# High-part casts and half of the second-key one-hots on ScalarE, every retrieval dot product on VectorE, and one-hot operands laid out by token pairs

## The chip, the core and the metric

The kernel runs on one NeuronCore of a Trainium2 chip. The core has five engines with an instruction queue each: TensorE (PE in the profile, its weight loads PEld), VectorE (DVE), ScalarE (ACT), GpSimd (POOL) and SyncE (SP), which issues plain DMA transfers. Each engine works through its queue strictly in the order in which the program was written. The metric is the device time of one launch in microseconds (us), the median of several runs.

## The reference

The block takes 512 tokens of width 1024 through a gated token mixer (a pooling branch and a gated delta rule with 8 heads) and then through PEER, a feed-forward layer of 16384 experts with one neuron each. The change touches PEER and the conversions of weights:

```python
q = (x @ w_query).reshape(b, s, 8, 2, 128)
s1 = einsum("bshc,hkc->bshk", q[..., 0, :], keys_1)   # 128 first keys for each head
s2 = einsum("bshc,hkc->bshk", q[..., 1, :], keys_2)   # 128 second keys
v1, i1 = top_k(s1, 16);  v2, i2 = top_k(s2, 16)
# 256 candidate sums v1 + v2, the best 16 of them; expert = i1 * 128 + i2
gates = softmax(top_score)
u  = take(expert_down, experts);  act = gelu(einsum("td,thkd->thk", x, u))
vv = take(expert_up, experts);    y = einsum("thk,thkd->td", gates * act, vv)
out = rmsnorm(h + y)
```

For each token 8 heads pick 16 experts each: 128 pairs of a first and a second key with a gate.

## The kernel before

**Two ways through PEER.** The tokens run in two segments, tokens 0 to 127 and tokens 128 to 511 (`SEGMENTS`, line 59). For the first 256 tokens (two tiles of 128) `retrieve` (line 1020) fetches the rows of the chosen experts: GpSimd issues an indirect DMA of 128 rows (512 KB) for each of the 128 picks, first from `down`, then from `up`. A `down` row goes into a dot product with the token (`tensor_tensor_reduce` on VectorE, CUSTOM_DVE in the profile); an `up` row is added to the tile `hbuf` with its weight (`scalar_tensor_tensor`). Only four buffers `rows` hold fetched rows. In the first tile, `SHARED` gives one dot product in sixteen, eight in all, to GpSimd (a product) and ScalarE (its sum).

**The dense way.** The last 256 tokens go through all 16384 experts (`dense`, line 1056), 128 experts at a time, in 128 steps. A step loads 512 KB of `downt` and 512 KB of `up`; `activations` (line 1093) multiplies the tokens with the first and applies Gelu, `add_up` (line 1110) multiplies by the gates and adds the product with the second into four accumulators. 28 steps of the first kind and 32 of the second take fp32 operands as they are. In the others `split` (line 561) makes a high part (`whi`, a cast to fp32r) and a low part (`wlo`, the difference, on VectorE), and TensorE runs three fp32r products for one. A high part may be cast by ScalarE or VectorE. There are three buffers each for `whi` and `wlo`.

**One-hots.** `gates_of_experts` (line 1062) builds the gate of every expert for every token with products of one-hot matrices, four tokens (`HOTS`) at a time: `o2` [pick, 128 second keys, 4 tokens] says which second key a pick has, `o1` [pick, 4 kinds, N first keys, 4 tokens] holds the same for a range of N first keys and that times the three bf16 pieces of the gate. For each token TensorE loads `o2[:, :, k]` and streams `o1[:, u, :, k]`, three matmuls. Neighbouring columns of these operands lie 4 elements, 8 bytes, apart. It runs in three passes (`PASSES`, line 33): 48 first keys before the dense steps begin, 32 between steps 17 and 46, 48 between steps 48 and 78, each of 64 groups of four tokens. VectorE makes a group in three instructions (`is_equal` for `o2`, `is_equal` for `o1`, a product).

**What sets the order.** The program first records all operations, then `Order.schedule` (line 287) lays them out with a cost for each kind of operation (`_cost`, line 243), a due time (`nc.vt`) and the state of the buffers, and writes each engine's queue in that order. Where `either` (line 202) names two engines, the planner picks one. Any change of a cost or an engine can therefore move instructions all over the program.

Of the kernel before, what the change touches and what calls it, by code (L numbers as in the profile page):

```python
# [13 lines left out]
BF16 = mybir.dt.bfloat16  # L14
I32 = mybir.dt.int32
U32 = mybir.dt.uint32
# [5 lines left out]
P = 128  # L22
# [14 lines left out]
HOTS = 4  # L37
# [11 lines left out]
WHOLE = range(16,80,2)  # L49
SHARED = ((1, 1, 1, 1, 1, 1, 1, 1), (0, 0, 0, 0, 0, 0, 0, 0))  # L50
BIASES = (1, 0.8, 0.6, -0.2, 1.5)
# [461 lines left out]
def block_kernel(ctx: ExitStack, tc: tile.TileContext, x, win, wbd, poolw, wpu, wdn, wmo, wq, down, up, downt,  # L513
# [25 lines left out]
    def psum():  # L539
        return bank([P, 512])  # L540
# [20 lines left out]
    def split(src, dst):  # L561
        copy(dst[0], src)
        if len(dst) == 1:
            return
        hi, lo = dst
        if src.slot.psum:
            nc.vector.tensor_tensor(lo, src, hi.bitcast(F32), op=ALU.subtract)
        else:
            sub(lo, src, hi.bitcast(F32))
# [23 lines left out]
    nc.gpsimd.iota(pari, pattern=[[0, P]], base=0, channel_multiplier=1)  # L593
    rowx = const([P, P, HOTS], BF16)
    nc.vector.tensor_copy(rowx, rowi[:, :, None].to_broadcast([P, P, HOTS]))
    masks = []
# [275 lines left out]
    def finish_tokens(t0, T, mg, exact):  # L872
# [41 lines left out]
        for c in range(16):  # L914
# [12 lines left out]
            for j in range(NT):  # L927
# [4 lines left out]
                top16(sc, VI[j][:, 0, c, :], VI[j][:, 1, c, :].bitcast(U32))  # L932
        bT = const([P, 5, TB], BF16) if any(kept) else None
        for j in range(first):
            vt, nc.vt = nc.vt, max(nc.vt, LATE) if any(kept) else nc.vt
            found = select(VI[j][:, 0], VI[j][:, 1].bitcast(U32), None)
            retrieve(t0 // P + j, *found, x2[j], hs[j])
            nc.vt = vt
        for j in range(first, NT):
            select(VI[j][:, 0], VI[j][:, 1].bitcast(U32), bT[:, :, (j - first) * P:(j - first + 1) * P])  # L940
        if any(kept):
            return bT, hs[first:], x2w[1], parted

# [7 lines left out]
    def select(V, I, slots):  # L951
# [39 lines left out]
        if slots is None:  # L991
            pt, idx = psum()[:, :P], keep([P, P], I32)
            for k in range(2 * TOPK):
                nc.tensor.matmul(pt, times[k // TOPK], hits[k // TOPK][:, k % TOPK, :],
                                 start=k == 0, stop=k == 2 * TOPK - 1)
            nc.vector.tensor_copy(idx, pt)
            return idx, gate
        for s in range(2):
            pt = psum()[:, :P]
            for k in range(TOPK):  # L1000
                nc.tensor.matmul(pt, hits[s][:, k, :], times[1], start=k == 0, stop=k == TOPK - 1)
            copy(slots[:, s, :], pt)
        pt = psum()[:, :P]
        nc.tensor.transpose(pt, gate, ident)
# [15 lines left out]
    def retrieve(j, idx, gate, x2, h):  # L1020
        act, co, shared = keep([P, P]), keep([P, P]), SHARED[j]

# [18 lines left out]
        for b in range(P // GROUP):  # L1041
            pace(b)
            for e in range(b * GROUP, (b + 1) * GROUP):
                row = gather(down, e)
                if e % GROUP * shared[b] // GROUP != (e % GROUP + 1) * shared[b] // GROUP:
                    nc.gpsimd.tensor_tensor(row, row, x2, op=ALU.mult)
                    nc.scalar.activation(row, row, AF.Copy, accum_out=act[:, e:e + 1])
                    continue
                nc.vector.tensor_tensor_reduce(out=row, in0=row, in1=x2, scale=1.0, scalar=0.0,
                                               op0=ALU.mult, op1=ALU.add, accum_out=act[:, e:e + 1])  # L1050
            if b:
                spread(b - 1)
# [3 lines left out]
    def dense(bT, hs, plain, x2w):  # L1056
# [4 lines left out]

        def gates_of_experts(first, N, n, place, *_):
            pieces = [pair([P, PIECE, TB]) if q < n else quads([P, PIECE, TB], at=place) for q in range(N // PIECE)]
# [3 lines left out]
            for t1 in range(0, TB, tb):  # L1067
                pg = bank([P, tb, N])
                for t in range(t1, t1 + tb, HOTS):
                    ts = slice(t, t + HOTS)  # L1070
                    o1, o2 = scr([P, 4, N, HOTS], BF16), scr([P, P, HOTS], BF16)
                    nc.vector.tensor_tensor(o2, rowx, bT[:, 1, None, ts].to_broadcast([P, P, HOTS]), op=ALU.is_equal)
                    nc.vector.tensor_tensor(o1[:, 0], rowx[:, first:first + N, :],
                                            bT[:, 0, None, ts].to_broadcast([P, N, HOTS]), op=ALU.is_equal)
                    nc.vector.tensor_tensor(o1[:, 1:], o1[:, 0:1].to_broadcast([P, 3, N, HOTS]),
                                            bT[:, 2:5, None, ts].to_broadcast([P, 3, N, HOTS]), op=ALU.mult)
                    for k in range(HOTS):
                        for u in range(1, 4):
                            nc.tensor.matmul(pg[:, t - t1 + k, :], o2[:, :, k], o1[:, u, :, k], start=u == 1, stop=u == 3)
                banks.append(len(nc.ops) - 1)  # L1080
# [43 lines left out]
        for e in range(NKEYS):  # L1124
            for k, (first, N, n, place, begin, end) in enumerate(PASSES):
                if e == begin:
                    build.append(gates_of_experts(first, N, n, place))
                if begin <= e <= end:
# [246 lines left out]
```

## Time and profile before

| what | value |
|---|---|
| median of 3 runs | 1857.65 us (1850.95 to 1860.94) |
| profiled execution | 1861.2 us, span of its instructions 1859.4 us |
| TensorE busy, granted clock | 1735.3 us (93%), 0.963 |
| VectorE busy | 1576.5 us (85%) |
| GpSimd busy | 771.0 us (41%) |
| ScalarE busy | 704.6 us (38%) |
| DMA | 509.31 MB, mean 274 GB/s |

The second segment begins at about 200 us. From about 250 us on the retrieval of the first tile runs beside it. The key scores and the selection of the last three token tiles lie between 750 and 966 us. The three one-hot passes run on TensorE from 966 to 1046 us, 1108 to 1297 us and 1313 to 1530 us; the dense steps go on to 1828 us, and beside them the second tile is retrieved.

Busy times of one engine count a moment once, even where its instructions overlap. A group line of the profile gives the busy time of all its instructions, the mean duration of one, and the idle time of the engine just before them with what ended it. All operations are issued through one helper, so that every one of them has line L494; the names of the tiles tell them apart.

### The profile page before, as it was taken

How to read it: one execution, taken by the hardware profiler on the slowest of the kernel's cores; microseconds unless marked ns; L12 is line 12 of the kernel's file. 1: busy time of each engine (PE TensorE's matmuls, PEld its weight loads, DVE VectorE, ACT ScalarE, POOL GpSimd, SP SyncE). 2: the span in 40 equal slices, each digit the busy share in tenths (PEclk: the TensorE clock that was granted, in tenths of full speed). 3: DMA queues.
4: the chain of work that ended last, by engine and by line, in shares of the span. 5: the costliest groups of instructions: out<-in, count | busy, mean ns of one | idle time of the engine just before them, and what ended most of it. 6: DMA issues, size and time to landing. Idle time of an engine off the chain costs nothing.

```text
span 1859.4 us, 33378 instructions
## 1 busy us (share of the span) xinstructions
PE 1735.3 (93%) x12122; PEld 1497.1 (81%) x12122; DVE 1576.5 (85%) x3832; ACT 704.6 (38%) x1688; POOL 771.0 (41%) x607
## 2 busy tenths in 40 slices
PE   7999999999999999899959998899999999999992
PEld 7999789999998874788748865687788878898981
DVE  5531398988987776899979999898999999999996
ACT  6741247747534220321213432233334433232331
POOL 0010026565556555533252254444554455334354
PEclk9999999998999999999979999899999999999996
DMA  7438757576677999877576599888998999999996
GB/s 247 153 120 281 252 187 254 182 255 199 210 242 242 335 318 356 294 237 262 192 251 198 169 372 316 315 289 321 327 336 321 327 320 355 317 333 348 333 353 235
DMA packets 144741, 509.31 MB, mean 274 GB/s; under 512 B 16961, under 2 KB 21185, under 8 KB 144577
## 3 DMA queue, kind: packets, MB, share of 16 engines
q0 software_dynamic: 73728, 268.47, 42.1%
q1 hardware_dynamic: 70848, 238.72, 36.6%
q8 instruction: 95, 1.56, 0.3%
q14 instruction: 70, 0.57, 0.1%
HBM read 505.02 MB, written 2.10 MB: 273 GB/s over the span
## 4 chain that ended last, share of the span: by engine, by line
PE 41%; DVE 21%; issue 15%; DMA 12%; POOL 8%; ACT 3%; POOLq 0%; SPq 0%; DVEq 0%; ACTq 0%
PE bank L494 41%; POOL rows L494 7%; DMA rows<-in_up_dram,keep 6%; DMA rows<-in_down_dram,keep 4%; DVE quad L494 4%; DVE rows L494 4%; DVE wlo L494 3%; DVE hbuf L494 3%; DVE scr L494 3%; DVE sel L494 2%; ACT L494 1%; DMA wraw<-in_win_dram 1%; DMA wraw<-in_downt_dram 1%; ACT scr L494 1%; DMA sel<-in_wq_dram 1%
## 5 line engine op out<-in xcount | busy, mean ns | idle before, releaser
L494 PE MATMUL bank<-xwide,whi 128*128 128x256 f32 (+1 forms) x2432 | 553.5, 313 | 0.9 <-DVE whi L494 0.7
L494 POOL DMA_INDIRECT rows<-in_down_dram,keep x256 | 316.9, 1238 | 474.8 <-DVE keep L494 340.3
L494 POOL DMA_INDIRECT rows<-in_up_dram,keep x256 | 360.5, 1408 | 361.1 <-DVE hbuf L494 198.5
L494 PEld LDWEIGHTS bank<-xwide,whi 128*128 128x128 f32 x2432 | 416.9, 195 | 8.7 <-issue 2.2
L494 PE MATMUL bank<-xwide,wlo 128*128 128x256 f32 (+1 forms) x1216 | 379.3, 312 | 13.9 <-DVE wlo L494 13.0
L494 ACT CAST whi<-wraw 128x512 fp32r<-128x512 f32 x406 | 251.0, 621 | 328.8 <-PE bank L494 269.1
L494 DVE SCALAR_TENSOR_TENSOR hbuf<-rows,keep,hbuf 128x1024 f32<-128x1024 f32 x256 | 329.8, 1288 | 45.7 <-DMA rows<-in_up_dram,keep 44.5
L494 DVE TENSOR_TENSOR wlo<-wraw,whi 128x512 fp32r<-128x512 f32 x496 | 341.9, 704 | 15.4 <-ACT whi L494 13.6
L494 DVE CUSTOM_DVE_ANT_0 rows<-rows,xbuf 128x1024 f32<-128x1024 f32 x248 | 304.3, 1232 | 43.2 <-DMA rows<-in_down_dram,keep 42.9
L494 PE MATMUL bank<-pair,wraw 128*128 128x128 f32 (+1 forms) x1728 | 259.5, 304 | 3.0 <-ACT pair L494 1.3
L494 PEld LDWEIGHTS bank<-xwide,wlo 128*128 128x128 f32 x1216 | 237.1, 195 | 26.1 <-DVE wlo L494 21.1
L494 PEld LDWEIGHTS bank<-pair,wraw 128*128 128x128 f32 x1728 | 223.0, 196 | 27.3 <-ACT pair L494 1.6
L494 PE MATMUL bank<-whi,xwide 128*128 128x512 f32 x768 | 238.4, 397 | 2.4 <-DVE xwide L494 0.9
L494 PE MATMUL bank<-quad,wraw 128*128 128x256 f32 x704 | 175.8, 394 | 0.0
L494 PEld LDWEIGHTS bank<-whi,xwide 128*128 128x128 f32 x768 | 138.7, 189 | 33.4 <-DVE xwide L494 2.9
L494 PE MATMUL bank<-wlo,xwide 128*128 128x512 f32 x384 | 147.2, 399 | 3.8 <-DVE wlo L494 3.6
L494 PEld LDWEIGHTS <-scr 128*128 128x128 bf16 x2304 | 110.5, 118 | 46.9 <-issue 31.8
L494 PEld LDWEIGHTS bank<-quad,wraw 128*128 128x128 f32 x704 | 130.1, 196 | 17.6 <-issue 3.0
L494 PE MATMUL bank<-scr 128*128 128x48 bf16 (+1 forms) x2304 | 120.5, 214 | 15.5 <-DVE scr L494 14.6
L494 DVE TENSOR_TENSOR scr<-c,c 128x512 bf16<-128x512 bf16 (+2 forms) x384 | 114.2, 330 | 5.3 <-PE bank L494 4.3
L494 POOL TENSOR_TENSOR small<-small,c 128x1 f32<-128x1 f32 (+1 forms) x20 | 22.2, 1109 | 181.1 <-DVE small L494 93.7
L494 PE MATMUL bank<-wraw,acts 128*128 128x512 f32 x208 | 96.2, 602 | 0.0
(160 smaller groups left out, 2081.6 us busy)
## 6 DMA issues: line engine op xcount, KB each, us to landing
wraw<-in_downt_dram SPq DMA_DIRECT2D x128, 512.0 KB
wraw<-in_up_dram SPq DMA_DIRECT2D x128, 512.0 KB
wraw<-in_win_dram SPq DMA_DIRECT2D x104, 512.0 KB
wraw<-in_wq_dram SPq DMA_DIRECT2D x32, 512.0 KB
wraw<-in_wdn_dram SPq DMA_DIRECT2D x16, 512.0 KB
wraw<-in_wmo_dram SPq DMA_DIRECT2D x16, 512.0 KB
wraw<-in_wpu_dram SPq DMA_DIRECT2D x8, 512.0 KB
rows<-in_down_dram,keep POOLq DMA_INDIRECT x256
```

Source lines behind the costliest of these rows:

```text
L494: ins = getattr(getattr(self.nc, eng), meth)(*(real(a) for a in args), **{k: real(a) for k, a in kw.items()})
```

## The change

`split` casts the high part on ScalarE always. `SHARED` is gone, so that all 256 dot products run on VectorE. `rowx`, `o1` and `o2` hold the tokens by pairs, so that neighbouring columns of an operand lie 2 elements, 4 bytes, apart; the product for `o1` becomes two instructions, one for each pair. In every second group (`SHARE`, 8 of 16) ScalarE makes `o2`: for each token |second key − row| by `Abs` with the key as bias, and then one `Relu` of 1 − that over the whole group. For it `select` leaves the second keys in fp32 as well (`bF`).

```diff
-SHARED = ((1, 1, 1, 1, 1, 1, 1, 1), (0, 0, 0, 0, 0, 0, 0, 0))
+SHARE = (8, 8, 8)
...
     def split(src, dst):
-        copy(dst[0], src)
+        nc.scalar.copy(dst[0], src)
...
+        slots, wide_slot = slots
         for s in range(2):
...
             copy(slots[:, s, :], pt)
+            if s:
+                copy(wide_slot, pt)
...
                 row = gather(down, e)
-                if e % GROUP * shared[b] // GROUP != (e % GROUP + 1) * shared[b] // GROUP:
-                    nc.gpsimd.tensor_tensor(row, row, x2, op=ALU.mult)
-                    nc.scalar.activation(row, row, AF.Copy, accum_out=act[:, e:e + 1])
-                    continue
                 nc.vector.tensor_tensor_reduce(out=row, in0=row, in1=x2, scale=1.0, scalar=0.0,
...
+        def pairwise(ap, n):
+            rows_of = ap.rearrange("p u (g t) -> p u g t", t=2)
+            return rows_of[:, :, :, None, :].to_broadcast([P, ap.shape[1], HOTS // 2, n, 2])
...
-                    o1, o2 = scr([P, 4, N, HOTS], BF16), scr([P, P, HOTS], BF16)
-                    nc.vector.tensor_tensor(o2, rowx, bT[:, 1, None, ts].to_broadcast([P, P, HOTS]), op=ALU.is_equal)
-                    nc.vector.tensor_tensor(o1[:, 0], rowx[:, first:first + N, :],
-                                            bT[:, 0, None, ts].to_broadcast([P, N, HOTS]), op=ALU.is_equal)
-                    nc.vector.tensor_tensor(o1[:, 1:], o1[:, 0:1].to_broadcast([P, 3, N, HOTS]),
-                                            bT[:, 2:5, None, ts].to_broadcast([P, 3, N, HOTS]), op=ALU.mult)
+                    o1, o2 = scr([P, HOTS // 2, 4, N, 2], BF16), scr([P, HOTS // 2, P, 2], BF16)
+                    if t // HOTS * share // 16 != (t // HOTS + 1) * share // 16:
+                        for k in range(HOTS):
+                            nc.scalar.activation(o2[:, k // 2, :, k % 2], rowx[:, :, 0], AF.Abs, scale=-1.0,
+                                                 bias=bF[:, t + k:t + k + 1])
+                        nc.scalar.activation(o2, o2, AF.Relu, scale=-1.0, bias=1.0)
+                    else:
+                        nc.vector.tensor_tensor(o2, rowx[:, None].to_broadcast([P, HOTS // 2, P, 2]),
+                                                pairwise(bT[:, 1:2, ts], P)[:, 0], op=ALU.is_equal)
+                    nc.vector.tensor_tensor(o1[:, :, 0], rowx[:, None, first:first + N, :].to_broadcast([P, HOTS // 2, N, 2]),
+                                            pairwise(bT[:, 0:1, ts], N)[:, 0], op=ALU.is_equal)
+                    for k in range(HOTS // 2):
+                        nc.vector.tensor_tensor(o1[:, k, 1:], o1[:, k, 0:1].to_broadcast([P, 3, N, 2]),
+                                                pairwise(bT[:, 2:5, ts], N)[:, :, k], op=ALU.mult)
                     for k in range(HOTS):
                         for u in range(1, 4):
-                            nc.tensor.matmul(pg[:, t - t1 + k, :], o2[:, :, k], o1[:, u, :, k], start=u == 1, stop=u == 3)
+                            nc.tensor.matmul(pg[:, t - t1 + k, :], o2[:, k // 2, :, k % 2], o1[:, k // 2, u, :, k % 2],
+                                             start=u == 1, stop=u == 3)
```

The planner lays out a new order. Three places of it follow. In their names `c_86` is `rowx`, `c_106` is `bT` and `c_107` is `bF`; `ISA rows,keep<-rows,xbuf` is a dot product of the retrieval.

VectorE, the end of the selection for the last token tile. Before, after the `RECIPROCAL` of the softmax:

```order
L494 TENSOR_REDUCE small<-sel 128x8
L494 TENSOR_TENSOR scr<-c_86,c_106 128x192
L494 RECIPROCAL small<-small 128x8
L494 ISA rows,keep<-rows,xbuf 128x1024
L494 ISA keep 128x1
...
L494 SCALAR_TENSOR_TENSOR hbuf<-rows,keep,hbuf 128x1024 x2
L494 TENSOR_TENSOR keep<-sel,small 128x128
L494 SCALAR_TENSOR_TENSOR hbuf<-rows,keep,hbuf 128x1024
L494 CAST c_106<-sel 128x128
```

Now:

```order
L494 TENSOR_REDUCE small<-sel 128x8
L494 SCALAR_TENSOR_TENSOR quad<-sel 128x128 x15
L494 RECIPROCAL small<-small 128x8
L494 TENSOR_TENSOR scr<-c_86,c_106 128x2x96
L494 TENSOR_TENSOR keep<-sel,small 128x128
L494 TENSOR_TENSOR scr<-c_86,c_106 128x2x96 x2
L494 SCALAR_TENSOR_TENSOR hbuf<-rows,keep,hbuf 128x1024
L494 CAST c_106<-sel 128x128
```

Before, twelve dot products of the first tile and two additions stood between the reciprocal and the gate (`keep<-sel,small`); now one one-hot does, and all 128 dot products of that tile stand ahead of the selection of the last tile.

ScalarE, in the first one-hot pass. Before, its queue held the three copies that move a finished group of gates out of PSUM, and now and then a Gelu:

```order
L494 ACTIVATE quad<-bank 128x256
L494 COPY pair<-bank 128x16x8 x6
L494 ACTIVATE quad<-bank 128x256
L494 COPY pair<-bank 128x16x8 x9
L494 ACTIVATE quad<-bank 128x256
```

Now:

```order
L494 ACTIVATE scr<-c_86,c_107 128x128 x4
L494 COPY pair<-bank 128x16x8 x3
L494 ACTIVATE scr<-scr 128x512
L494 ACTIVATE scr<-c_86,c_107 128x128 x3
L494 ACTIVATE quad<-bank 128x256
L494 ACTIVATE scr<-c_86,c_107 128x128
L494 COPY pair<-bank 128x16x8 x3
L494 ACTIVATE scr<-scr 128x512
```

Between two sets of three copies stand four `Abs` and a `Relu`.

VectorE, the end of the program. Before:

```order
L494 COPY wraw<-bank 128x512
L494 SCALAR_TENSOR_TENSOR hbuf<-rows,keep,hbuf 128x1024
L494 TENSOR_SCALAR small<-small 128x1
L494 SCALAR_TENSOR_TENSOR hbuf<-rows,keep,hbuf 128x1024 x7
L494 SCALAR_TENSOR_TENSOR wraw<-wraw,small,rows 128x1024
L494 SCALAR_TENSOR_TENSOR xbuf<-hbuf,small,rows 128x1024
```

Now:

```order
L494 SCALAR_TENSOR_TENSOR xbuf<-hbuf,small,rows 128x1024
L494 TENSOR_TENSOR wlo<-wraw,whi 128x512 x2
L494 TENSOR_TENSOR acts<-acts,quad 128x256
L494 TENSOR_TENSOR xwide<-acts,xwide 128x256
L494 TENSOR_TENSOR wlo<-wraw,whi 128x512 x4
L494 COPY wraw<-bank 128x512 x4
L494 SCALAR_TENSOR_TENSOR wraw<-wraw,small,rows 128x1024 x2
```

The retrieved tile's last step (`xbuf<-hbuf`) was the last instruction of all; now it stands ahead of the last low parts of the dense steps, and the dense tokens end the queue.

## Rows read from the trace of the kernel before

**Rows 1.** The page, busy time of each engine over the span.
```profile
PE 1735.3 (93%) x12122; PEld 1497.1 (81%) x12122; DVE 1576.5 (85%) x3832; ACT 704.6 (38%) x1688; POOL 771.0 (41%) x607
```

**Rows 2.** Windows: us, busy by engine (instructions), granted clock, DMA share, GB/s.
```profile
650.00:700.00 50.00, 49.11 (x206) 36.73 (x205) 37.03 (x44) 9.72 (x16) 27.76 (x21) 1.00 0.91 323
966.00:1046.00 80.00, 76.51 (x930) 67.50 (x931) 76.69 (x208) 25.18 (x108) 18.93 (x15) 0.91 0.54 173
1046.00:1828.00 782.00, 751.03 (x5314) 614.77 (x5312) 757.90 (x1489) 280.37 (x631) 364.94 (x262) 0.98 0.92 326
1108.00:1297.00 189.00, 174.39 (x1448) 131.76 (x1448) 178.53 (x408) 57.31 (x127) 82.53 (x68) 0.95 0.88 312
1297.00:1530.00 233.00, 229.41 (x1840) 184.98 (x1839) 225.99 (x459) 92.71 (x240) 115.30 (x81) 1.00 0.93 328
1530.00:1700.00 170.00, 166.54 (x1029) 145.88 (x1026) 167.33 (x296) 57.61 (x120) 76.41 (x55) 0.99 0.94 340
1828.00:1859.00 31.00, 0.00 (x0) 0.00 (x0) 16.31 (x17) 3.63 (x7) 11.64 (x9) 0.51 0.65 232
```

**Rows 3.** Timeline around the selection's end: start, us, instruction, [idle before and releaser].
```profile
929.66 0.20 DVE L494 RECIPROCAL small<-small 128x8 f32<-128x8 f32 x1
941.95 1.23 DVE L494 CUSTOM_DVE_ANT_0 rows<-rows,xbuf 128x1024 f32<-128x1024 f32 x1 [3.29 <-DMA rows<-in_down_dram,keep]
...
962.17 0.28 DVE L494 TENSOR_TENSOR keep<-sel,small 128x128 f32<-128x128 f32 x1
...
962.50 0.47 PE L494 MATMUL bank<-c,keep 128*128 128x128 f32 x1 [13.63 <-DVE keep L494]
```

**Rows 4.** Timeline of PE: one-hot matmuls, each run with its follower, and fp32r matmuls.
```profile
1005.82 0.73 PE L494 MATMUL bank<-scr 128*128 128x48 bf16 x12
1006.37 0.68 PE L494 MATMUL bank<-quad,wraw 128*128 128x256 f32 x2
...
1033.09 0.28 PE L494 MATMUL bank<-xwide,wlo 128*128 128x256 f32 x1
1033.21 0.40 PE L494 MATMUL bank<-xwide,whi 128*128 128x256 f32 x2
...
1157.15 0.55 PE L494 MATMUL bank<-scr 128*128 128x32 bf16 x12
1157.55 0.48 PE L494 MATMUL bank<-whi,xwide 128*128 128x512 f32 x1
```

**Rows 5.** Groups by form: count | busy us, mean ns | idle before and releasers.
```profile
L494 DVE TENSOR_TENSOR scr<-c,c 128x512 bf16<-128x512 bf16 x192 | 80.2, 419 | 5.3 <-PE bank L494 4.3
L494 DVE TENSOR_TENSOR scr<-scr,c 128x576 bf16<-128x576 bf16 x128 | 57.2, 449 | 0.0
L494 DVE TENSOR_TENSOR scr<-scr,c 128x384 bf16<-128x384 bf16 x64 | 22.3, 349 | 0.0
L494 DVE TENSOR_TENSOR scr<-c,c 128x192 bf16<-128x192 bf16 x128 | 32.3, 252 | 0.0
L494 DVE CAST whi<-wraw 128x512 fp32r<-128x512 f32 x90 | 38.1, 428 | 6.2 <-PE bank L494 5.0 <-DMA wraw<-in_downt_dram 1.2
L494 DVE CUSTOM_DVE_ANT_0 rows<-rows,xbuf 128x1024 f32<-128x1024 f32 x248 | 304.3, 1232 | 43.2 <-DMA rows<-in_down_dram,keep 42.9
L494 POOL TENSOR_TENSOR rows<-rows,xbuf 128x1024 f32<-128x1024 f32 x8 | 19.5, 2434 | 7.5 <-DMA rows<-in_down_dram,keep 7.5
L494 ACT CAST whi<-wraw 128x512 fp32r<-128x512 f32 x406 | 251.0, 621 | 328.8 <-PE bank L494 269.1 <-DMA wraw<-in_up_dram 14.8 <-issue 11.0
L494 ACT ACTIVATE quad<-quad,small 128x128 f32<-128x128 f32 x16 | 5.3, 389 | 0.0
L494 ACT ACTIVATE quad<-quad 128x512 f32<-128x512 f32 x8 | 5.0, 626 | 0.4 <-DVE quad L494 0.4
L494 ACT COPY pair<-bank 128x128 f32<-128x128 f32 x160 | 33.2, 272 | 97.7 <-PE bank L494 97.5
```

**Rows 6.** Timeline, the end of the program.
```profile
1845.65 2.65 DVE L494 SCALAR_TENSOR_TENSOR hbuf<-rows,keep,hbuf 128x1024 f32<-128x1024 f32 x2 [2.97 <-DMA rows<-in_up_dram,keep]
...
1852.70 0.33 SPq L494 DMA_DIRECT2D out_dram<-xbuf  x1
```

More of the change, by code (lines that the diff above doesn't have):

```diff
@@ L593, in block_kernel @@
     nc.gpsimd.iota(pari, pattern=[[0, P]], base=0, channel_multiplier=1)
-    rowx = const([P, P, HOTS], BF16)
-    nc.vector.tensor_copy(rowx, rowi[:, :, None].to_broadcast([P, P, HOTS]))
+    rowx = const([P, P, 2], BF16)
+    nc.vector.tensor_copy(rowx, rowi[:, :, None].to_broadcast([P, P, 2]))
     masks = []
@@ L933, in finish_tokens @@
         bT = const([P, 5, TB], BF16) if any(kept) else None
+        bF = const([P, TB]) if any(kept) else None
         for j in range(first):
@@ L939, in finish_tokens @@
         for j in range(first, NT):
-            select(VI[j][:, 0], VI[j][:, 1].bitcast(U32), bT[:, :, (j - first) * P:(j - first + 1) * P])
+            select(VI[j][:, 0], VI[j][:, 1].bitcast(U32), (bT[:, :, (j - first) * P:(j - first + 1) * P], bF[:, (j - first) * P:(j - first + 1) * P]))
         if any(kept):
-            return bT, hs[first:], x2w[1], parted
+            return (bT, bF), hs[first:], x2w[1], parted
     def top16(sc, v, i):
@@ L1020, in retrieve @@
     def retrieve(j, idx, gate, x2, h):
-        act, co, shared = keep([P, P]), keep([P, P]), SHARED[j]
+        act, co = keep([P, P]), keep([P, P])
         def pace(b):
@@ L1060, in dense, with gates_of_experts @@
         where = {}
-        def gates_of_experts(first, N, n, place, *_):
+        bT, bF = bT
+        def pairwise(ap, n):
+            rows_of = ap.rearrange("p u (g t) -> p u g t", t=2)
+            return rows_of[:, :, :, None, :].to_broadcast([P, ap.shape[1], HOTS // 2, n, 2])
+        def gates_of_experts(first, N, n, place, share):
             pieces = [pair([P, PIECE, TB]) if q < n else quads([P, PIECE, TB], at=place) for q in range(N // PIECE)]
@@ L1126, in dense @@
                 if e == begin:
-                    build.append(gates_of_experts(first, N, n, place))
+                    build.append(gates_of_experts(first, N, n, place, SHARE[k]))
                 if begin <= e <= end:
```

## The prediction

> **What bounds the kernel now.** I read the busy times first, then windows by stage, then the timelines where an engine stands still. TensorE is busy 93% of the span and VectorE 85% [rows 1], but these are means over unlike stages. The stretch that decides runs from the end of the first one-hot pass to the last matmul, 1046 to 1828 us. There VectorE is busy 757.9 of 782 us, TensorE 751 of 782, and the DMA engines 0.92 at 326 GB/s [rows 2]: three resources close to full, so relief for one is worth only what the next leaves. ScalarE is busy 280 of 782 and GpSimd 365. The reader should also see the 31 us after it, in which TensorE has nothing and VectorE waits for the last fetched rows [rows 2, 6]: the retrieval of the second tile, not the dense steps, ends the program. One plain stall stands earlier: between the reciprocal at 929.66 and the gate at 962.17 us lie twelve dot products that wait for their rows, one by one (3.29 us in the case shown), and TensorE then stands still for 13.63 us for that gate [rows 3].
>
> **VectorE.** It loses 90 casts of high parts, 38.1 us [rows 5], and gains eight dot products of 1.23 us, 9.9 us. One-hots: an `o2` costs 80.2/192 = 0.418 us, an `o1` of 192 elements 0.252, the product of 576 elements 57.2/128 = 0.447. A product of 288 lies between the rows of 192 (0.252) and 384 (0.348), 0.300. Two groups with 48 keys cost 2 × (0.418 + 0.252 + 0.447) = 2.23 us and will cost 0.418 + 2 × 0.252 + 4 × 0.300 = 2.12; with 32 keys the difference is −0.418 + 4 × 0.252 − 2 × 0.348 = −0.11 as well. Splitting the product eats nearly all that ScalarE takes over: 96 pairs of groups save about 11 us. In all VectorE loses some 39 us: 44 after 1046 us, where 87 of the 90 casts and two of three passes lie, against 5 more before. GpSimd loses eight products, 19.5 us [rows 5].
>
> **ScalarE.** The nearest row to an `Abs` with a bias per partition is the scaled copy from SBUF to SBUF, four in a row: 5.3/16 = 0.33 us each; to the `Relu`, the 512-element operation of 0.626 us [rows 5]. A group is 4 × 0.33 + 0.63 = 1.95 us, 96 of them 187 us, and 90 casts of 0.62 add 56 us. In the first pass 32 groups add 62 us to 25.2 busy in a window of 80 [rows 2]: 87.6 us. There ScalarE becomes the bound and the pass grows by up to 8 us; if VectorE and the fp32 matmuls queued beside it absorb that, by nothing. I take +6. In the second pass it has 57 + 62 of 189 us, in the third 93 + 62 of 233 [rows 2]: room.
>
> **TensorE.** Twelve one-hot matmuls with 48 columns take 1006.37 − 1005.82 = 0.55 us, 46 ns each; with 32 columns 0.40 us, 33 ns each. The difference, 12.5 ns for 16 columns, is 0.78 ns a column, where a fp32r matmul of 256 columns follows the one before it in 0.12 us, 0.47 ns a column [rows 4]. The fp32r columns lie 4 bytes apart, those of the one-hots 8. By bytes the new operands stand where fp32r stands, so I expect the matmuls with 48 columns to drop from 46 ns towards 0.47 × 48 = 23 ns; as no pair of load and matmul in these rows is quicker than 33 ns, I take 33 and nothing for 32 columns. That is 1536 × 12.5 ns = 19 us, half of it in the third pass; the bounds are 0 and 1536 × 23 + 768 × 18 ns = 49 us.
>
> The Trainium skill, SBUF — State Buffer, Specifications (TRN2), speaks against this: it says that lines of 16 bytes need two hits each for full bandwidth, and 8-byte steps already give two. The trace disagrees as far as it goes, 0.78 against 0.47 ns. By the page the layout brings TensorE nothing, which is the rival "no faster" below.
>
> **The stall before the pass.** In the new order one one-hot stands between reciprocal and gate. The 13.63 us go if the twelve dot products find room earlier; VectorE has it where it is busy 37 of 50 us, but transfers are at 0.91 there [rows 2, 3]. Between 0 and −14 us; I take −10. What covers it is that slack; if it is gone, the wait for rows simply moves up. The eight added dot products and the reshuffled queues of the first 930 us: 0 to +10, I take +3, since the same room hides them.
>
> **The dense stretch to the end**, 813 us with the tail. Three floors. VectorE: 757.9 + 16.3 = 774 us busy, less 44, at its present share of 757.9/782: 45 us shorter. TensorE: 10 us from the third pass, and of its 31 us without work two thirds, which I put down to VectorE being late: 31 us. Transfers: 782 × 0.326 + 31 × 0.232 = 262 MB; at 340 GB/s, the rate of 1530 to 1700 us, 771 us, plus the 12 us from the last row's landing to the end [rows 2, 6], 783 against 813: 30 us. The shortest gain counts: −30. That needs the retrieval to end inside the dense steps, as the new order has it; then the 31 us tail shrinks to the 12 us or so of the last normalisation. Bounds: 0 (the transfers do not go faster than 326) and −45.
>
> **Sum.** −10 + 3 + 6 − 30 = −31 on the profiled execution's own 1861.2 us: 1830. The median of the runs is 3.5 us lower: **1827 us**.
>
> **Rivals.**
> - *The transfers hold.* The weights and the gathers are at 0.92 to 0.94 [rows 2] and do not move faster than 326 GB/s; then the relieved VectorE waits for rows instead of working. For it: the last additions wait 2.97 us for a row [rows 6]. Against: 340 GB/s over 170 us. The stretch stays 813 us: 1858 − 10 + 3 + 6 = 1857.
> - *One-hots no faster on TensorE.* Its gain in the stretch falls to the 21 us of waits: 1836.
> - *ScalarE late (slower).* A cast of a high part queues behind a one-hot group, 1.95 us, three copies of gates (33.2/160 = 0.21 us each), a Gelu and another cast, about 3.6 us. Cover: two other `whi` buffers, each 12 matmuls of 0.12 us, 2.9 us. From more than 2.9 us in front of a cast on, TensorE waits: 0.7 us and up to a cast's 0.6 more, 64 groups in passes two and three, some 40 to 80 us, against a gain of about 20 left after 1530 us: 1857 + 45 − 20 = about 1882. Against it: ScalarE would be only two thirds full there, and the planner spaces its queue.
> - *VectorE loses its double rate on pairs.* The bf16 rows give (0.447 − 0.252)/384 = 0.51 ns an element. If runs of two elements made that 1.02, the 96 `o2`, 192 `o1` and 384 products, about 180,000 elements, would cost 92 us more; two thirds of it less 44 in the stretch, the rest in the first pass: about 1896. For it: no row has runs of two. Against: a pair of bf16 is one 4-byte word, and the runs of four already share the rate.
> - *Everything gives way.* VectorE's full 45 us, the whole stall, nothing lost in pass one: 1858 − 14 − 45 = about 1797.
>
> **How the numbers follow.** Forecast 0.47; transfers hold 0.18; no faster on TensorE 0.12; ScalarE late 0.12; single rate 0.04; everything 0.07. A difference under 0.5%, 9 us, cannot be told from none. Faster: 0.47 + 0.12 + 0.07 + 0.05 of the transfers' case = 0.71; same: 0.12 of that case; slower: 0.16 + 0.01 = 0.17. The range holds all but the two slower mechanisms and the far end of the last case: 1796 to 1862.
>
> **What would show it.** VectorE busy about 1537 us, ScalarE about 705 + 187 + 56 − 8 = 940. A run of twelve matmuls with 48 columns in 0.40 us or less. No wait of TensorE over 10 us before the first pass, and that pass 85 to 88 us long with ScalarE full. After it a DMA rate above 335 GB/s, and the last matmul within some 12 us of the end. I am wrong if VectorE is less busy but waits for rows as long as it gained, if casts on ScalarE end TensorE's waits, or if a product of 288 takes 0.45 us.

## The result, and the profile after

The changed kernel takes 1799.61 us (median of 4 runs, 1790.64 to 1800.56), the kernel before 1855.47 (4 runs): a ratio of 0.969, 95% interval [0.965, 0.973], some 56 us. The forecast was 1827, 27 us too high; the direction was right. The profiled execution spans 1798.8 us after 1859.4.

The page's busy times after, to be read against [rows 1]:

```profile
PE 1693.2 (94%) x12122; PEld 1453.4 (81%) x12122; DVE 1528.5 (85%) x3858; ACT 903.0 (50%) x2248; POOL 736.6 (41%) x596
```

VectorE does 48 us less, TensorE 42, ScalarE 198 more. I cut both programs at the same four marks: the first one-hot matmul, the end of the first pass, the end of the third pass, the last matmul. Each window is of one execution, and the runs of the changed kernel lie up to 10 us apart, so a difference of a few us in one stretch decides nothing. Windows of the kernel before: us, busy time of PE, PEld, DVE, ACT, POOL (instructions), granted clock, DMA share, GB/s.

```profile
966.60:1046.30 79.70, 76.78 (x936) 67.76 (x937) 76.39 (x207) 25.18 (x108) 18.34 (x15) 0.91 0.54 172
1046.30:1530.30 484.00, 464.62 (x3564) 363.97 (x3561) 464.05 (x968) 180.12 (x426) 227.28 (x167) 0.97 0.91 320
1530.30:1827.80 297.50, 286.06 (x1749) 250.51 (x1746) 293.35 (x521) 100.05 (x205) 137.58 (x96) 0.99 0.93 335
1827.80:1859.40 31.60, 0.05 (x1) 0.00 (x0) 16.51 (x17) 3.83 (x7) 11.72 (x10) 0.51 0.65 229
```

The same four stretches after the change:

```profile
946.80:1036.40 89.60, 78.31 (x1009) 63.37 (x1008) 83.24 (x252) 80.47 (x274) 58.04 (x26) 0.96 0.73 246
...
1493.70:1786.70 293.00, 282.15 (x1752) 250.18 (x1748) 268.68 (x421) 144.08 (x295) 117.28 (x90) 1.00 0.93 339
1786.70:1798.80 12.10, 0.00 (x0) 0.00 (x0) 3.48 (x6) 2.19 (x4) 2.09 (x2) 0.60 0.21 87
```

```profile
1036.40:1493.70 457.30, 433.18 (x3544) 331.06 (x3540) 444.58 (x1032) 284.95 (x747) 208.49 (x164) 1.00 0.92 333
```

The first pass begins 19.8 us sooner and takes 9.9 us longer, with ScalarE busy 80 of 90 us; passes two and three, with the steps around them, take 26.7 us less; the steps behind them 4.5 less; the tail 19.5 less. Together 60.6. In passes two and three VectorE is 96% busy before and 97% after. Behind them it was 99% busy and is now 92%: there something else has become the bound. TensorE is 96% busy there, as before. The chain of waits (start, us, what) has TensorE alone from there on, ten blocks of 144 matmuls and one of 147, with less than 1 us between two:

```profile
1519.55 22.93 PE bank L494 x144
1543.45 22.93 PE bank L494 x144
...
1758.56 26.07 PE bank L494 x147
```

What ends these waits is a cast on ScalarE. From 1493.7 to 1786.7 us (us in total, times, longest):

```profile
PE bank L494 <- ACT whi L494: 10.8, 11, 1.0
```

That is all the time that TensorE stands without work there; before it was 11.4 us, most of it waits for low parts from VectorE.

The end of the selection, where TensorE had waited 13.63 us [rows 3], in the timeline of DVE and of PE (start, us, instruction, idle time before it where there was any):

```profile
939.45 0.19 DVE L494 RECIPROCAL small<-small 128x8 f32<-128x8 f32 x1
939.56 0.20 DVE L494 TENSOR_TENSOR scr<-c,c 128x192 bf16<-128x192 bf16 x1
939.74 0.29 DVE L494 TENSOR_TENSOR keep<-sel,small 128x128 f32<-128x128 f32 x1
```

```profile
940.18 1.08 PE L494 MATMUL bank<-quad,wraw 128*128 128x256 f32 x4
941.10 0.27 PE L494 MATMUL bank<-c,keep 128*128 128x128 f32 x1
```

Reciprocal to gate takes 0.3 us instead of 32, and TensorE does not wait. The one-hot matmuls, against [rows 4]:

```profile
960.71 0.77 PE L494 MATMUL bank<-scr 128*128 128x48 bf16 x24
961.31 0.68 PE L494 MATMUL bank<-quad,wraw 128*128 128x256 f32 x2
```

```profile
1104.78 0.45 PE L494 MATMUL bank<-scr 128*128 128x32 bf16 x12
1105.08 1.10 PE L494 MATMUL bank<-wraw,quad 128*128 128x512 f32 x2
```

24 of 48 columns in 0.60 us, 12 of 32 in 0.30: 25 ns each, at either width, where they took 46 and 33. The groups that answer to [rows 5]:

```profile
L494 DVE CUSTOM_DVE_ANT_0 rows<-rows,xbuf 128x1024 f32<-128x1024 f32 x256 | 316.0, 1241 | 27.6 <-DMA rows<-in_down_dram,keep 27.2
L494 ACT CAST whi<-wraw 128x512 fp32r<-128x512 f32 x496 | 301.4, 621 | 213.5 <-PE bank L494 165.7 <-DVE wlo L494 13.4 <-DMA wraw<-in_downt_dram 8.3
L494 ACT ACTIVATE scr<-c,c 128x128 bf16<-128x128 bf16 x384 | 137.7, 441 | 43.6 <-PE bank L494 42.2 <-DVE scr L494 1.0
L494 DVE TENSOR_TENSOR scr<-scr,c 128x288 bf16<-128x288 bf16 x256 | 65.6, 301 | 0.4
L494 ACT ACTIVATE scr<-scr 128x512 bf16<-128x512 bf16 x96 | 61.5, 640 | 1.1
L494 DVE TENSOR_TENSOR scr<-c,c 128x512 bf16<-128x512 bf16 x96 | 40.0, 417 | 0.2
L494 DVE TENSOR_TENSOR scr<-scr,c 128x192 bf16<-128x192 bf16 x128 | 26.0, 247 | 0.0
```

And the end, against [rows 6]: the last addition to the retrieved tile starts at 1764.32 us, 22 us ahead of the last matmul instead of 19 behind it, and the dense tokens end the program.

```profile
1764.32 1.28 DVE L494 SCALAR_TENSOR_TENSOR hbuf<-rows,keep,hbuf 128x1024 f32<-128x1024 f32 x1
...
1790.76 1.28 DVE L494 SCALAR_TENSOR_TENSOR wraw<-wraw,small,rows 128x1024 f32<-128x1024 f32 x1 [0.44 <-POOL small L494]
```

### The profile page after: what moved, and what is told of

The parts are those of the page before. It is cut to its first block, busy times and chain, and to the rows that moved or that the text cites. A ratio compares the mean times of both kernels' runs of the same rounds, so it can differ in the third digit from the quotient of the medians.

```text
span 1798.8 us, 33982 instructions
## 1 busy us (share of the span) xinstructions
PE 1693.2 (94%) x12122; PEld 1453.4 (81%) x12122; DVE 1528.5 (85%) x3858; ACT 903.0 (50%) x2248; POOL 736.6 (41%) x596
## 4 chain that ended last, share of the span: by engine, by line
PE 29%; DVE 22%; DMA 14%; issue 10%; POOL 3%; ACT 1%; POOLq 0%; ACTq 0%; DVEq 0%
PE bank L494 29%; DMA rows<-in_up_dram,keep 9%; DVE scr L494 5%; DVE rows L494 4%; DVE hbuf L494 4%; DVE wlo L494 3%; DVE quad L494 3%; DMA rows<-in_down_dram,keep 3%; POOL rows L494 3%; DVE sel L494 2%; DMA wraw<-in_downt_dram 1%; DVE acts L494 1%; ACT whi L494 1%; DMA wraw<-in_win_dram 0%; DVE xwide L494 0%
## 5 line engine op out<-in xcount | busy, mean ns | idle before, releaser
L494 PE MATMUL bank<-xwide,whi 128*128 128x256 f32 (+1 forms) x2432 | 540.3, 308 | 0.6 <-ACT whi L494 0.6
L494 POOL DMA_INDIRECT rows<-in_down_dram,keep x256 | 305.6, 1194 | 427.6 <-DVE keep L494 281.0
L494 PEld LDWEIGHTS bank<-xwide,whi 128*128 128x128 f32 x2432 | 408.5, 191 | 6.9 <-ACT whi L494 1.6
L494 ACT CAST whi<-wraw 128x512 fp32r<-128x512 f32 x496 | 301.4, 621 | 213.5 <-PE bank L494 165.7
L494 PE MATMUL bank<-xwide,wlo 128*128 128x256 f32 (+1 forms) x1216 | 373.2, 307 | 11.3 <-DVE wlo L494 11.2
L494 DVE CUSTOM_DVE_ANT_0 rows<-rows,xbuf 128x1024 f32<-128x1024 f32 x256 | 316.0, 1241 | 27.6 <-DMA rows<-in_down_dram,keep 27.2
L494 PE MATMUL bank<-whi,xwide 128*128 128x512 f32 x768 | 240.5, 398 | 13.5 <-ACT whi L494 10.8
L494 ACT ACTIVATE scr<-c,c 128x128 bf16<-128x128 bf16 x384 | 137.7, 441 | 43.6 <-PE bank L494 42.2
L494 PEld LDWEIGHTS <-scr 128*128 128x128 bf16 x2304 | 73.8, 97 | 54.7 <-issue 30.0
L494 PEld LDWEIGHTS bank<-wlo,xwide 128*128 128x128 f32 x384 | 72.1, 188 | 31.1 <-DVE wlo L494 16.0
L494 PE MATMUL bank<-scr 128*128 128x48 bf16 (+1 forms) x2304 | 80.3, 182 | 17.8 <-DVE scr L494 13.2
```

The costliest lines, as they stand in the source:

```text
L494: ins = getattr(getattr(self.nc, eng), meth)(*(real(a) for a in args), **{k: real(a) for k, a in kw.items()})
```

## The experiments

I set three theories against each other. Theory A: TensorE bounds the stretch from the first pass to the last matmul and its faster one-hot matmuls made the gain. Theory B: VectorE's work sets the end, and what ScalarE took over made it. Theory C: the new order did it, above all at the end of the selection.

All runs in one table; the ratio is to runs of the kernel before on the same chip. The last five columns are from each run's profiled execution (us): span, busy time of VectorE, first one-hot matmul, end of the third pass, and the time from there to the end of the program.

| run | median us | ratio, 95% interval | span | VectorE busy | pass 1 begins | pass 3 ends | rest |
|---|---|---|---|---|---|---|---|
| before | 1855.47 | | 1859.4 | 1576.5 | 966.6 | 1530.3 | 329.1 |
| changed | 1799.61 | 0.969 [0.965, 0.973] | 1798.8 | 1528.5 | 946.8 | 1493.7 | 305.1 |
| e1 before, pairs only | 1857.69 | 1.002 [0.999, 1.004] | 1856.3 | 1583.2 | 942.6 | 1523.1 | 333.2 |
| e2 changed, steps of 8 bytes | 1793.77 | 0.968 [0.966, 0.971] | 1789.7 | 1519.1 | 942.8 | 1484.9 | 304.8 |
| e3 changed, shared dots | 1799.39 | 0.970 [0.967, 0.974] | 1798.5 | 1521.7 | 954.0 | 1494.1 | 304.4 |
| e4 changed, casts on either | 1813.27 | 0.977 [0.975, 0.980] | 1815.7 | 1557.1 | 941.7 | 1491.6 | 324.1 |
| e5 changed, SHARE 0, 0, 0 | 1827.59 | 0.985 [0.980, 0.991] | 1825.0 | 1556.6 | 941.1 | 1519.9 | 305.1 |
| e6 before, casts only | 1800.69 | 0.972 [0.967, 0.978] | 1797.7 | 1543.7 | 923.0 | 1492.0 | 305.7 |
| e7 before, one-hots only | 1828.82 | 0.987 [0.982, 0.993] | 1825.8 | 1549.9 | 950.0 | 1504.9 | 320.9 |
| e8 SHARE 8, 12, 12 | 1786.55 | 0.965 [0.959, 0.971] | 1781.4 | 1516.6 | 940.2 | 1478.4 | 303.0 |
| e9 before, o1 product cut | 1825.63 | 0.984 [0.981, 0.987] | 1817.3 | 1549.1 | 949.8 | 1484.1 | 333.2 |
| e10 e8 with steps of 8 bytes | 1793.63 | 0.966 [0.963, 0.969] | 1792.7 | 1512.0 | 948.2 | 1489.9 | 302.8 |
| e11 changed, pairs in o2 alone | 1791.67 | 0.965 [0.962, 0.969] | 1788.1 | 1519.1 | 945.7 | 1482.7 | 305.4 |
| e12 SHARE 8, 16, 16 | 1786.97 | 0.963 [0.960, 0.966] | 1783.9 | 1509.2 | 945.1 | 1479.2 | 304.7 |
| e13 SHARE 0, 8, 8 | 1793.36 | 0.968 [0.966, 0.971] | 1792.4 | 1534.4 | 948.5 | 1486.7 | 305.7 |
| e14 SHARE 4, 12, 12 | 1787.30 | 0.963 [0.961, 0.966] | 1786.8 | 1521.6 | 948.2 | 1479.9 | 306.9 |

Span less VectorE's busy time lies between 254 and 283 us in all sixteen rows, while the busy time ranges over 74: that is theory B at first sight. The last column does not follow it: e5 has 305.1 us with VectorE busy for 1556.6 us, e7 320.9 with 1549.9. It follows the engine of the casts.

The runs come from several chips, on which the kernel before took 1851.7 to 1857.0 us (medians). Where two runs of different chips differ by less than 10 us, I compare their ratios.

**e1, the layout alone.** The kernel before with this, all `o2` on VectorE:

```diff
...
-o1, o2 = scr([P, 4, N, HOTS], BF16), scr([P, P, HOTS], BF16)
+o1, o2 = scr([P, HOTS // 2, 4, N, 2], BF16), scr([P, HOTS // 2, P, 2], BF16)
...
```

> The kernel before with the pair layout alone (two products of 288 for one of 576, operand columns 4 bytes apart); casts, shared dot products and second-key one-hots stay as they were. VectorE gets some 25 us more work (128 x 2 x 0.256 + 64 x 2 x 0.203 - 57.2 - 22.3 = +12 us at the least). Theory A, TensorE bounds the dense stretch and its one-hot matmuls were the loss: a run of twelve of 48 columns in 0.30 us, the whole at 1815 to 1830 us. Theory B, VectorE bounds it, and its relief by ScalarE made the gain: 1855 to 1875 us, since VectorE only gets more.

The same time as before, although VectorE's busy time grew by only 7 us, where 12 at the least were expected. Theory A falls. The windows of e1 show where the gain on TensorE went (first pass, passes two and three):

```profile
942.60:1012.70 70.10, 65.53 (x940) 51.74 (x938) 70.10 (x262) 25.26 (x108) 64.50 (x5) 1.00 0.36 124
1012.70:1523.10 510.40, 457.72 (x3564) 348.53 (x3560) 481.06 (x1104) 179.16 (x423) 241.88 (x177) 0.95 0.89 313
```

The first pass ends at 1012.7 us, 33.6 sooner, and VectorE is never idle in it. But passes two and three take 510 us for 484: VectorE has 17 us more to do there, TensorE has 53 us without work in them (19 before), and 7.2 of the 33.6 us are left. The new order at the end of the selection (24 us sooner) was given back as well: theory C alone is not enough. e1 takes load off TensorE and puts some on VectorE; a run with the first alone is missing.

**e2, the layout undone.** The changed kernel with `o1` and `o2` by four tokens, products whole.

> The changed kernel with the operands of the one-hot matmuls laid out by four tokens again, columns 8 bytes apart; casts, second-key one-hots on ScalarE and dot products as changed. Theory A: a run of twelve of 48 columns back at 0.55 us, 42 us more on TensorE, 1830 to 1842 us. Theory B: 1795 to 1812 us, as VectorE even saves the split of the product.

As theory B had it (1 us below its range), no slower than the changed kernel. The two passes:

```profile
1037.20:1484.90 447.70, 443.12 (x3508) 351.17 (x3505) 428.99 (x890) 305.47 (x739) 193.26 (x157) 1.00 0.92 330
```

TensorE is 99% busy, VectorE 96%; by pairs it was 95% and 97% of 457 us. In these two passes the layout takes 10 us from TensorE and gives VectorE 16, at a place where both are nearly full.

**e3, shared dot products back.** The changed kernel with the removed lines of `retrieve` again.

> The changed kernel with eight dot products of the first tile again made by GpSimd and ScalarE. Theory A and theory B: within 6 us of the changed kernel's 1800. Theory C, the order around the end of the selection made 20 us of the gain and comes from the eight dot products: 1812 to 1822 us, with a wait of TensorE of over 10 us before the first pass.

No difference, and no wait of TensorE of 5 us or more between 750 us and the first pass. The eight dot products cost nothing that shows, and did not make the wait.

**e4, casts on either engine.** The changed kernel with

```diff
-        nc.scalar.copy(dst[0], src)
+        copy(dst[0], src)
```

> The changed kernel with the planner choosing the engine of the high-part casts again, VectorE or ScalarE. Theory A: within 8 us of 1800, faster if anything, as the waits of TensorE and VectorE for a cast (25 us in front of low parts) get shorter. Theory B: some 35 us of VectorE work come back, 1815 to 1830 us.

13.7 us slower, a little less than theory B's range. The table says where: the third pass ends no later (1491.6), but the rest takes 324 us for 305. The planner puts nearly all of VectorE's casts there, 93 of 106 in e4:

```profile
L494 DVE CAST whi<-wraw 128x512 fp32r<-128x512 f32 x93 | 38.6, 423 | 0.1
```

Groups of the kernel before, from 1530.3 us to the end:

```profile
L494 ACT CAST whi<-wraw 128x512 fp32r<-128x512 f32 x107 | 66.4, 621 | 79.3 <-PE bank L494 72.1 <-DVE wlo L494 2.7 <-issue 1.7
L494 DVE CAST whi<-wraw 128x512 fp32r<-128x512 f32 x85 | 36.0, 428 | 1.2 <-PE bank L494 1.2
```

There 85 of the 90 casts, 36 us, stand in the last 329 us.

**e5, no one-hots on ScalarE.** The changed kernel with `SHARE = (0, 0, 0)`.

> The changed kernel with all second-key one-hots on VectorE again (SHARE 0, 0, 0); pairs, casts on ScalarE and dot products as changed. VectorE gets 96 x 0.417 = 40 us back, some 30 of it after the first pass. Theory B (VectorE's work sets the end): 1825 to 1840 us, VectorE busy about 1568. Theory A' (the freed TensorE and the casts made the gain): 1795 to 1810 us.

28 us slower than the changed kernel, all of it before the third pass ends (1519.9 for 1493.7 us); the rest is 305.1 in both. Passes two and three alone take 39 us more, 496.2 for 457.3.

**e6, casts alone.** The kernel before with the one line of e4 the other way round.

> The kernel before with the high-part casts on ScalarE alone. VectorE loses 38 us. Theory B: 1815 to 1830 us, TensorE still at 46 ns a one-hot matmul. Rival, ScalarE late: at 1850 us or above, with waits of TensorE for casts.

The edit of one line brings what the whole change brings, more than theory B gave it. 23.4 us lie behind the third pass (305.7 for 329.1), as in e4. The other 38 lie ahead of it, where VectorE had five casts in all, some 2 us. So they must come from the order: the first pass begins 43.6 us sooner. Between 750 us and the pass VectorE is idle for 5.8 us, before for 21.6, and it has 28 us less work there, which the planner put elsewhere (the windows of e6, of before and of the changed kernel):

```profile
750.00:923.00 173.00, 163.53 (x976) 143.56 (x977) 167.16 (x808) 41.49 (x118) 58.98 (x45) 0.99 0.71 236
```

```profile
750.00:966.60 216.60, 187.68 (x1067) 163.22 (x1066) 195.03 (x839) 52.32 (x136) 87.76 (x67) 0.93 0.73 247
```

```profile
750.00:946.80 196.80, 182.54 (x1032) 156.28 (x1031) 183.50 (x833) 49.36 (x131) 76.44 (x56) 0.97 0.72 244
```

Why the planner's order is that much better here I have not settled. e1 also began 24 us sooner and kept 7. So order, theory C, has a share that these runs do not separate.

**e7, one-hots alone.** The kernel before with half of `o2` made by ScalarE, by four tokens.

> The kernel before with half of the second-key one-hots on ScalarE alone (laid out by four tokens; casts on either engine, eight shared dot products). VectorE loses 40 us. Theory B: 1815 to 1830 us. Together with the run on casts alone the two gains should add up to about 60 us if VectorE alone bounds, to clearly more than 60 if TensorE or the transfers stop the run that has both.

27 us, in the range; 25.4 of the profiled 33.6 us come before the third pass ends. The two gains add up to 55 + 27 = 82 us, and e2, which has both, gained 61. That does not show that TensorE or the transfers stop it. The shortfall lies ahead of the first pass, which e6 begins 43.6 us sooner, e7 16.6 and e2, with both, only 23.8. In passes two and three e2 gains 36 us, more than e6 (3) and e7 (22) together.

**e8, a larger share.** The changed kernel with `SHARE = (8, 12, 12)`.

> The changed kernel with three quarters of the second-key one-hots of passes two and three on ScalarE (SHARE 8, 12, 12). VectorE loses 32 x 0.417 = 13 us more. Theory B: 1785 to 1793 us. If TensorE or the transfers already bound the stretch: 1796 to 1802. If ScalarE comes late: over 1802, with waits of TensorE for casts.

1786.55 us, in theory B's range: 13 us below the changed kernel by the medians, 7 by the ratios, whose intervals overlap (0.959 to 0.971 and 0.965 to 0.973). So the gain is likely and not shown. Passes two and three:

```profile
1031.20:1478.40 447.20, 431.00 (x3546) 331.62 (x3542) 430.58 (x997) 335.56 (x907) 210.84 (x161) 1.00 0.94 337
```

**e9, less work for VectorE and none for others.** The kernel before with

```diff
-nc.vector.tensor_tensor(o1[:, 1:], o1[:, 0:1].to_broadcast([P, 3, N, HOTS]),
+nc.vector.tensor_tensor(o1[:, 1:2], o1[:, 0:1],
...
-nc.tensor.matmul(pg[:, t - t1 + k, :], o2[:, :, k], o1[:, u, :, k], start=u == 1, stop=u == 3)
+nc.tensor.matmul(pg[:, t - t1 + k, :], o2[:, :, k], o1[:, 1, :, k], start=u == 1, stop=u == 3)
```

> The kernel before with the product of o1 made for one of the three pieces of the gate (192 elements for 576, 128 for 384; all three matmuls read that piece, so the gates lack the other two). VectorE does about 34 us less before the end of the third pass; casts, TensorE, ScalarE and GpSimd stay. Stage theory (VectorE bounds the passes, the casts after the third pass bound the end): passes end 20 to 35 us sooner, from the end of the third pass to the end of the program 321 to 333 us as before, in all 1820 to 1835 us. Rival, a cast made on VectorE costs more than its duration anywhere and other VectorE work costs less: within 10 us of 1855.

VectorE's busy time falls by 27 us, the median by 31, and the third pass ends 46 us sooner in the profiled execution; the rest takes 333 us. 17 of the 46 us are an earlier first pass, 29 come after its start. A gain before the third pass needs no lighter work for TensorE and no help from ScalarE, and it does not shorten the rest. Passes two and three:

```profile
1028.40:1484.10 455.70, 448.04 (x3549) 353.60 (x3547) 440.17 (x970) 176.30 (x421) 221.38 (x163) 1.00 0.93 334
```

TensorE has the same work as before here, and yet it is busy for 448 us instead of 465: the granted clock is 1.00, where it was 0.97. So a part of what VectorE's relief brings comes as a higher clock: if all of TensorE's work followed the clock, 465 us would become 465 × 0.97 = 451, by this estimate at most some 14 of the 28 us. TensorE is without work for 8 us instead of 19. In the changed kernel the clock of these passes is 1.00 too, with 24 us without work; in e1, with 53, it is 0.95. No run holds the clock fixed, so the two shares are not separated.

**e10 and e11, what the step does.** e8 with both operands by four tokens, and the changed kernel with `o2` alone by pairs.

> The changed kernel with columns 8 bytes apart and three quarters of the second-key one-hots of passes two and three on ScalarE. Stage theory: TensorE had no idle time in passes two and three of the run with 8-byte steps and half on ScalarE, so nothing is gained over its 1794: 1789 to 1798 us, where the pair layout with the same share took 1787. If VectorE alone bounds: 1778 to 1785.

> The changed kernel with o2, which TensorE loads, by pairs, and o1, which it streams, by four tokens with one product. If the streamed columns' step sets the matmul's time: twelve of 48 columns in 0.55 us, and a time like the run with 8-byte steps, 1790 to 1797. If the loaded operand's step sets it: 0.30 us and, as VectorE saves the split, 1783 to 1792.

e10 gained nothing over e2, as expected. e8 is 7 us faster than e10, but their ratios to before overlap (0.959 to 0.971, 0.963 to 0.969), and passes two and three last 447.2 and 448.3 us: a gain of the layout is not shown. In e11 the matmuls are as slow as before: it is not the loaded operand's step that sets their time. With the changed kernel, where both are laid out by pairs, that leaves the streamed operand's step, alone or with the other; the streamed operand alone by pairs was not run. The timeline of PE in e11:

```profile
961.71 0.72 PE L494 MATMUL bank<-scr 128*128 128x48 bf16 x12
962.25 1.11 PE L494 MATMUL bank<-quad,wraw 128*128 128x256 f32 x4
...
1101.73 0.55 PE L494 MATMUL bank<-scr 128*128 128x32 bf16 x12 [0.47 <-DVE scr L494]
1102.11 1.10 PE L494 MATMUL bank<-wraw,quad 128*128 128x512 f32 x2
```

Twelve in 0.54 us, 45 ns each; with 32 columns in 0.38 us, 32 ns each.

**e12 to e14, other shares.** `SHARE = (8, 16, 16)`, then, since ScalarE is busy for 90% of the first pass and whether that costs the end was still open, `(0, 8, 8)` and `(4, 12, 12)`.

> The changed kernel with all second-key one-hots of passes two and three on ScalarE (SHARE 8, 16, 16). VectorE loses 13 us more than with 12. Stage theory: TensorE had 16 us without work in passes two and three there, so 1775 to 1785 us; if ScalarE comes late, over 1787, with longer waits of TensorE for casts.

> The changed kernel with all second-key one-hots of the first pass on VectorE (SHARE 0, 8, 8), 32 x 0.417 = 13 us more for it. If the longer first pass (90 us for 80) costs the end what it lasts: the pass back to 72 to 82 us and the whole at 1788 to 1795 us. If VectorE's work alone decides: the pass is shorter and the whole 1805 to 1815 us.

> The changed kernel with a quarter of the second-key one-hots of the first pass and three quarters of those of passes two and three on ScalarE (SHARE 4, 12, 12). Against the run with 8, 12, 12 (1787 us) VectorE has 7 us more, ScalarE 33 us less in the first pass. If the first pass counts: 1778 to 1785; if VectorE's work alone: 1790 to 1796.

e12 gained nothing over e8, 2 us above its first range, and passes two and three take 444.6 us for 447.2:

```profile
1034.60:1479.20 444.60, 430.31 (x3544) 333.79 (x3540) 426.75 (x969) 382.97 (x1067) 204.45 (x165) 0.98 0.95 344
```

TensorE is 97% busy, VectorE 96, the DMA engines 95: all three are nearly full. TensorE's longest waits there are now for one-hots from ScalarE, 7.7 us in all, where they were 0.6 in the changed kernel. In e13 the first pass is back to 82 us, and the whole is 6 us faster than the changed kernel by the medians, but the same by the ratios (0.968 and 0.969), although VectorE does 6 us more; e14 against e8 shows nothing. Whether the longer first pass costs the end stays open.

## Why the prediction was wrong

**What bounds the kernel: right, and then used wrongly.** VectorE, TensorE and transfers were named as close to full after the first pass. The experiments show two stretches. Until the third pass ends, VectorE's work sets the time: less of it shortens the kernel before (e9), more of it lengthens the changed kernel (e5), and the layout, which relieves TensorE, gains nothing (e1). TensorE is close behind, 99% busy in e2. From there to the end VectorE with its 85 casts was the bound, and the retrieval came late. The ten experiments with every cast on ScalarE take 303 to 307 us there, the changed kernel 305; all kernels with casts on both take 321 to 333. The gap is what the casts brought: 24 us against the kernel before, 19 against e4, 16 between e7 and e2. Of the 24 us only 4.5 are dense steps, in which TensorE is busy 96% of the time before and after; 19.5 are the tail that the late retrieval made.

**The dense stretch, −30: the step that failed.** Measured from the end of the first pass to the end of the program: 813.1 to 762.4 us, −50.7. Its working had two errors, both in how the floors were set.
- *The transfers' floor.* The shortest of the three gains was 262 MB at 340 GB/s. The rate was as taken (333 and 339 GB/s), but the amount was not: 457.3 × 0.333 + 293.0 × 0.339 + 12.1 × 0.087 = 253 MB. The first pass, ten us longer and at 246 GB/s for 172, carried 22.0 MB for 13.7, so 8 of the 9 MB went ahead. An amount that fetches may move across the border of a window is no floor for that window.
- *TensorE's floor.* Its 31 us were set against 813 us, but TensorE's work ends with the last matmul, 782 us on. To there the stretch fell from 781.5 to 750.3 us, 31.2, the number of the sum; the tail's 19.5 come on top: 50.7. The prediction itself had the tail at 12 us, and it is 12.1.

That 31 came out right was luck: its parts did not. Of the 31 us without work two thirds were to go, and none did: TensorE stands without work for 35.0 us now, 30.8 before. Its busy time fell by 35 us instead of 10, a part of it at a granted clock of 1.00 for 0.97 and 0.99. The one-hot matmuls take 25 ns, not 33, at either width: 2304 of them save 1536 × 21 + 768 × 8 ns = 38 us where 19 were taken, inside the bounds of 0 to 49. The rule of the Trainium skill, SBUF — State Buffer, Specifications (TRN2), two hits in a line of 16 bytes for full bandwidth, is contradicted for these matmuls: steps of 8 bytes have them and cost 46 ns, steps of 4 bytes 25. But no gain in time came of it, with the work it gives VectorE (e1, e2). I sized a saving on an engine that was waiting for another.

**VectorE, −39: 48.** Casts as computed. The dot products +11.7 against +9.9. The one-hots gave the difference: the halves of the product take 65.6/256 = 0.256 and 26.0/128 = 0.203 us, not 0.300 and 0.252. The split costs 65.6 + 26.0 − 57.2 − 22.3 = 12 us, and the `o2` that went save 40.2. The rate was kept: 0.053 us for 96 elements more, 0.55 ns each, where the rows before gave 0.51. (By these groups the change is some 58 us, by all groups 71; their instructions overlap at the ends, and VectorE's busy time counts that once.) Of the stretch alone VectorE lost 773.9 − 716.7 = 57, not 44: 128 of the 256 additions of fetched rows were done before it, where it had been 114.

**ScalarE.** A group costs 4 × 137.7/384 + 61.5/96 = 2.07 us, not 1.95. Busy 903 us, not 940. The first pass took 89.6 us, where ScalarE's work was to set 87.6 and the sum took +6: it grew by 9.9. ScalarE was busy for 80 of the 89.6, so it did not set the length alone; TensorE waited 9 us there for one-hots from VectorE. What the longer pass costs the end is open (e13).

**The stall, −10 and +3: too small.** The first pass begins 19.8 us sooner, not 7. The 13.63 us are gone, and VectorE is idle for 13.3 us between 750 us and the pass, for 21.6 before. The reason given, the twelve dot products, holds for the place. But e1 and e3 keep the shared dot products and have no such wait either: it was a product of the old order, not of that part of the change. All fifteen other kernels begin the first pass 13 to 44 us sooner than the kernel before, whatever was edited, and e1 shows that such a start can be lost again.

**The rivals.** *The transfers hold*: refuted, they went ahead. *One-hots no faster*: refuted for the rate, and e2 shows that its price of 9 us was wrong too. *ScalarE late*: its 40 to 80 us are refuted, also at a share of 16, but not its mechanism, as the 10.8 us of waits for casts after the third pass show. *Single rate*: refuted. *Everything gives way* named the right time, 1797 (its terms give 1799): VectorE's full relief and the whole stall, though not its unchanged first pass. Start, pass and stretch were −14, 0 and −45 in it and are −19.8, +9.9 and −50.7: the errors cancel. Its chance of 0.07 was too low because the transfers' floor stood against it.

**The signs.** Four held: VectorE, the matmuls, no wait before the pass, the last matmul 12 us from the end. The pass was 1.6 us over its bound, and ScalarE was not full in it. ScalarE was 37 us below its figure; the DMA rate after the pass, 335 GB/s, stood at the bound. Of the three signs of being wrong one came true: after the third pass casts on ScalarE end TensorE's waits.

## What to carry to other kernels

When several engines are close to full, test each by taking load off it: here the faster matmul, with the work it gave VectorE, was worth nothing, and one line that moved casts was worth as much as the whole change, though 38 of its 62 us in the profile came with an order whose merit is unexplained. Set each floor against the stretch in which its resource works (TensorE's to the last matmul, then the tail), and ask whether transfers can leave the window before using their amount as a floor. Look at where in the program an engine's work stands, not only at its sum: 36 us of casts counted because 85 of 90 stood in the last stretch, where VectorE was 99% busy. The best versions run, with 12 or 16 of 16 `o2` of passes two and three on ScalarE, take 1787 us; e12 and e14 have ratios of 0.960 to 0.966 and 0.961 to 0.966 against 0.965 to 0.973 for the changed kernel.

## What the runs showed of the hardware

A matmul of 48 bf16 columns takes 46 ns with the streamed columns 8 bytes apart and 25 ns at 4 bytes; with 32 columns 33 and 25 ns. Laying out the loaded operand alone by 4 bytes moves it to 45 and 32 ns. That the time at 4 bytes is the same for 32 and 48 columns says that the columns no longer set it there; what does, the runs don't tell.

These are times at a granted clock of 1.00. At 0.50, the lower of the two levels (1.2 GHz for 2.4), the kernel before and the changed kernel have these runs of 24 matmuls with 48 columns:

```profile
970.38 1.32 PE L494 MATMUL bank<-scr 128*128 128x48 bf16 x24 [0.56 <-DVE scr L494]
971.52 1.20 PE L494 MATMUL bank<-quad,wraw 128*128 128x256 f32 x2
```

```profile
1015.48 1.17 PE L494 MATMUL bank<-scr 128*128 128x48 bf16 x24
1016.48 0.78 PE L494 MATMUL bank<-quad,wraw 128*128 128x256 f32 x1
```

At steps of 8 bytes a matmul takes 1.14/24 us, 48 ns, at half the clock, much as at the full one: there the clock does not set its time. At 4 bytes it takes 1.00/24 us, 42 ns, for 25: there the clock does.
